# A two-layer diffusion block on one core: the last feed-forward's way down with tokens as weights in four banks, modulation products in runs of four, and a longer matmul in the plan

## The chip, the cores and the metric

The kernel runs on one core of one Trainium2 chip. The metric is the device time in microseconds (us) of one execution; less is better. The profile follows one execution on that core, and its times count from the first instruction.

## The reference, cut to what matters

Two streams of 256 tokens by 1024 features, an image `x` and a context `ctx`, go through two layers. Layer 0 mixes with an mLSTM, layer 1 with neighbourhood attention; each layer then has a gated feed-forward with a short convolution. Shift, scale and gate of each sublayer come from a small product with `ada_w`, the modulation. Only `x` goes through layer 1's feed-forward.

```python
def conv_ffn(h, w_up, b_up, conv_w, conv_b, w_down, b_down):
    u = dwconv(h @ w_up + b_up, conv_w, conv_b)          # 1024 -> 2 x 2816
    a, g = jnp.split(u, 2, axis=-1)
    return (a * jax.nn.silu(g)) @ w_down + b_down          # 2816 -> 1024
...
mod_x = jnp.split((silu_c @ ada_w[i] + ada_b[i])[:, None, :], 6, axis=-1)
hx = modulate(rmsnorm(xx, norm2_g[i]), mod_x[3], mod_x[4])
xx = xx + mod_x[5] * conv_ffn(hx, ...)
...
return rmsnorm(xx, final_g)
```

## The kernel before, in words

**Layout.** Activations lie with features on the partitions and tokens along the free axis: `X[k]` is 128 features by 512 tokens, 256 of `ctx` and 256 of `x`. Float32 accuracy is had from TensorE's one-pass format (fp32r) by splitting each operand into a high and a low part: a cast on ACT writes the high part, a subtraction on DVE the low one (`split`, `split_w`), and `mm3` (line 473) issues three matmuls, high by high, high by low, low by high. A weight tile of 128 by 1024 is loaded to a raw buffer (three of them), cast and subtracted into one of five pairs of buffers. Small products, the modulation among them, are plain float32 matmuls with 32 columns of weights, four side by side on the array (a quad).

**Stages.** First the modulation for norm 1 (`first_scale`, line 505, with rows named `adc`, and `first_shift`, line 526, with rows named `adh`), while the first weights land. Then the mLSTM's projections `u`, its gates, and for each of four heads a front part, the decay matrices, the product `h`, the transposes `ht` (`heads_out`, line 1069) and the way out `wo`; tiles of the projection `z` are put between as filler. Then layer 0's feed-forward on 512 tokens, the attention of layer 1, and layer 1's feed-forward on 256 tokens.

**The modulation.** `ada_steps` (line 545) is a generator: each call of `trickle` does one slice of 128 features. Three of the units go through TensorE (rows `ada<-ra,sc_c`), a quad for each slice, when it has landed; the others are summed on DVE (`aa`) and end in a quad (rows `ada<-aa,esel`).

**The last feed-forward.** `feed_forward` (line 1136) takes the 22 tiles of hidden features in three blocks of 8, 8 and 6. A block is first made (`up` twice for each tile, then convolution taps, a product with silu and a split) and then taken down: for each of 8 output tiles, rows `dn`, weights are the 128 by 128 pieces of `ff_down`, and the hidden tile of 256 tokens moves. The result goes to `X[m]` with bias and gate (`residual`, line 1085). After the last block `finish` (line 1360) scales each output tile, squares it, and turns it with two transposes (`yt`) to tokens on partitions; sums of squares (`pmfin`) give the last norm, and four transfers write the output.

**Who sets the order.** Nothing is issued as written. `Plan.record` keeps each operation with a price (`cost`, line 145) and what it depends on; `group` makes several one. `run` then walks through a planned time with one queue for each engine, picks what is ready and due first, and writes the order down. The prices are fixed numbers, among them:

```python
            if ins[0].dtype == F32R:
                return max(n, 64) / 2.4 + 3, None
            ...
            return 0.833 * n + (52 if psum else 94) + extra, table      # ACT
        return 70 + scalars + (0.52 if fast else 1.04) * n, None        # DVE
```

At run time each engine works through its list in this order and waits where something is missing.

Of the kernel before, what the change touches and what calls it, by code (L numbers as in the profile page):

```python
# [9 lines left out]
F32 = mybir.dt.float32  # L10
F32R = mybir.dt.float32r
AF = mybir.ActivationFunctionType
ALU = mybir.AluOpType
# [44 lines left out]
Z_TILES = (((), (0, 1, 2, 3), (4,)), ((), (5, 6, 7), (8,)), ((), (9, 10, 11), (12,)), ((), (13, 14, 15), ()))  # L58
ADA_VECTOR = {(1, u) for u in range(6)} | {(0, 4)}


class Plan:
# [6 lines left out]
    DMA_RATE = 360.0  # L69
    AHEAD = 100000  # L70
# [14 lines left out]
    def __init__(self, nc, tc):  # L85
# [5 lines left out]
        self.seen = set()  # L91
        self.ops_engine = []
# [56 lines left out]
    def cost(engine, method, outs, ins, kw):  # L149
        n = max([x.free_size() for x in outs[:1] + ins[:1]])  # L150
        psum = any(x.space == bass.MemoryType.PSUM for x in ins)
        if engine == "tensor":
# [3 lines left out]
            if ins[0].dtype == F32R:  # L156
                return max(n, 64) / 2.4 + 3, None
# [22 lines left out]
    def add(self, engine, cost, ins, outs, fns, table, dma=False):  # L180
# [23 lines left out]
        for name, r, _, is_w in acc:  # L204
# [7 lines left out]
                             outs=outs, dma=dma, load=dma and outs[0].space != bass.MemoryType.DRAM))  # L212


    def run(self):
# [83 lines left out]
        while started < n:  # L299
            progress = True  # L300
            while progress:
                progress = False
                for e in avail:
# [32 lines left out]
                    if o["dma"]:  # L336
# [3 lines left out]
                        end = s + c  # L340
# [57 lines left out]
def diffusion_block(ctx: ExitStack, tc: tile.TileContext, I: dict, out: bass.AP):  # L398
# [80 lines left out]

    def split(src, name, n=T):  # L480

        hi = page("h" + name, F32R)
        lo = page("l" + name, F32R)
        nc.scalar.copy(out=hi[:, :n], in_=src)
        nc.vector.tensor_tensor(out=lo[:, :n], in0=src, in1=hi.bitcast(F32)[:, :n], op=ALU.subtract)
        return hi, lo
# [18 lines left out]
    def first_scale(q):  # L505

        ps = bank(f"adc{q}")
        for i in range(4):
            w = page(f"aq{q}{i}")
            load(w, I["ada0c"][q, i])  # L510
            with nc.group():
                for j in range(4):
                    k = i + 4 * (j // 2)
                    nc.tensor.matmul(ps[32 * j:32 * j + 32, :P], sc_c[:, 32 * k:32 * k + 32], w[:, P * j:P * j + P],
                                     start=i == 0, stop=i == 3)
# [10 lines left out]
    def first_shift(half):  # L526

        ps = bank(f"adh{half}")
        for k in range(KD):
            w = page(f"ah{half}{k}")  # L530
            load(w, I["ada0h"][half, k])
            with nc.group():
                for j in range(4):
                    nc.tensor.matmul(ps[32 * j:32 * j + 32, :P], sc_c[:, 32 * k:32 * k + 32],
                                     w[:, P * j:P * j + P], start=k == 0, stop=k == KD - 1)
# [9 lines left out]
    def ada_steps(l, u):  # L545
        ps = bank(f"ada{l}{u}") if (l, u) not in ADA_VECTOR else None
        only = [1] if l == 1 and u > 1 else [0, 1]
        acc = {}
        for k in range(KD):
            if ps is not None:  # L550
                w = raw_w(I["ada"][6 * l + u - 2, k], f"a{l}{u}{k}")
                with nc.group():
                    for j in range(4):
# [806 lines left out]
    def finish(k):  # L1360
# [16 lines left out]
        if k < KD - 1:  # L1377
            turn()
# [153 lines left out]
```

## Time and profile before

| | us |
|---|---|
| three runs | 1193.1, 1193.97, 1194.65 (median 1193.97) |
| the profiled execution's own time | 1195.27 |
| its span, first to last instruction | 1193.1 |
| TensorE (PE) busy | 1173.0 |
| VectorE (DVE) busy | 938.4 |
| ScalarE (ACT) busy | 679.9 |

A matmul's shown time is from its issue to its modelled end, so neighbours overlap; the distance between two starts is what one costs in a row of many. PEld is TensorE's weight load, which runs beside the matmuls. Nearly every instruction has line 137, since the plan issues it there; the names of tiles tell what it is. `sc_c`, `hdn`, `lup` are names of tiles: an `h` or `l` ahead is a high or low part, an `r` a raw load.

### The profile page before, as it was taken

What the parts mean: (1) busy time and instruction counts of PE and PEld (TensorE: products, weight loads), DVE (VectorE), ACT (ScalarE), POOL (GpSimd) and SP (SyncE); (2) the same over time, 40 slices, a digit from 0 to 9 for tenths busy, and PEclk for the clock granted to TensorE, in tenths of its full rate; (3) what the DMA queues carried; (4) which work ended last, traced back from release to release, by engine and by line L of the source; (5) the groups of instructions that cost most, each with busy time, mean ns of one, the idle gap of its engine ahead of it and who ended that gap; (6) DMA issues with size and microseconds to landing.
All of it is one profiled execution on the core that took longest, in us unless ns stands there. A gap on an engine that the chain in (4) does not pass through costs nothing.

```text
span 1193.1 us, 19033 instructions
## 1 busy us (share of the span) xinstructions
PE 1173.0 (98%) x7122; PEld 980.5 (82%) x7122; DVE 938.4 (79%) x1871; ACT 679.9 (57%) x1212; POOL 26.4 (2%) x59
## 2 busy tenths in 40 slices
PE   7999999999999999999999999999999999999997
PEld 4677777888878788878888888888788899999997
DVE  6898678867875699997897667687966879978675
ACT  4465675562735447553455325454857876867473
POOL 0000000000000000000000000000000000000000
PEclk9999999999999999999999999999999999999999
DMA  9647625413344406318457456422432432576552
GB/s 354 248 159 238 185 63 176 141 54 120 119 141 124 151 17 221 107 53 282 132 186 247 135 199 222 145 72 71 116 120 82 161 104 87 173 228 185 182 160 76
DMA packets 68636, 180.05 MB, mean 151 GB/s; under 512 B 8128, under 2 KB 10688, under 8 KB 68544
## 3 DMA queue, kind: packets, MB, share of 16 engines
q1 hardware_dynamic: 68544, 178.84, 46.2%
q8 instruction: 56, 0.92, 0.3%
q14 instruction: 36, 0.29, 0.1%
HBM read 174.61 MB, written 4.19 MB: 150 GB/s over the span
## 4 chain that ended last, share of the span: by engine, by line
PE 78%; issue 16%; DVE 3%; DMA 2%; ACT 1%; SPq 0%; POOL 0%; POOLq 0%; DVEq 0%; ACTq 0%
PE up L137 21%; PE dn L137 10%; PE u L137 8%; PE wo L137 7%; PE z L137 6%; PE k L137 4%; PE va L137 4%; PE h L137 3%; PE q L137 3%; PE sc L137 2%; PE no L137 2%; PE ada L137 2%; PE o L137 1%; PE pt L137 1%; PE s L137 1%
## 5 line engine op out<-in xcount | busy, mean ns | idle before, releaser
L137 PE MATMUL up<-hhn,hup 128*128 128x512 f32 (+1 forms) x640 | 215.9, 337 | 0.0
L137 PE MATMUL up<-hln,hup 128*128 128x512 f32 (+1 forms) x640 | 215.3, 336 | 0.3 <-DVE hln L137 0.3
L137 PE MATMUL up<-hhn,lup 128*128 128x512 f32 (+1 forms) x640 | 215.1, 336 | 0.0
L137 ACT CAST hup<-rup 128x1024 fp32r<-128x1024 f32 x80 | 83.7, 1050 | 128.6 <-PE up L137 64.7
L137 PEld LDWEIGHTS up<-hhn,hup 128*128 128x128 f32 x640 | 121.5, 190 | 14.0 <-issue 0.8
L137 PEld LDWEIGHTS up<-hln,hup 128*128 128x128 f32 x640 | 121.5, 190 | 12.8 <-DVE hln L137 0.5
L137 PEld LDWEIGHTS up<-hhn,lup 128*128 128x128 f32 x640 | 121.5, 190 | 12.5
L137 DVE TENSOR_TENSOR lup<-rup,hup 128x1024 fp32r<-128x1024 f32 x80 | 97.4, 1223 | 39.6 <-ACT hup L137 39.1
L137 PE MATMUL dn<-hhid,hdn 128*128 128x512 f32 (+1 forms) x352 | 119.3, 339 | 0.0
L137 PE MATMUL dn<-hhid,ldn 128*128 128x512 f32 (+1 forms) x352 | 118.4, 336 | 0.0
L137 PE MATMUL dn<-lhid,hdn 128*128 128x512 f32 (+1 forms) x352 | 118.4, 336 | 0.0
L137 DVE SCALAR_TENSOR_TENSOR fc<-fu,vec,fc 128x510 f32<-128x510 f32 (+1 forms) x176 | 104.6, 612 | 4.8 <-ACT fc L137 4.0
L137 DVE SCALAR_TENSOR_TENSOR aa<-ra,sc_c,aa 128x512 f32<-128x512 f32 x140 | 97.5, 745 | 4.5 <-DMA ra<-in_ada 4.3
L137 ACT CAST hdn<-rdn 128x1024 fp32r<-128x1024 f32 (+1 forms) x48 | 46.6, 979 | 46.5 <-PE up L137 27.1
L137 PEld LDWEIGHTS dn<-hhid,hdn 128*128 128x128 f32 x352 | 66.8, 190 | 7.6 <-issue 0.8
L137 PEld LDWEIGHTS dn<-hhid,ldn 128*128 128x128 f32 x352 | 66.8, 190 | 7.3 <-DVE ldn L137 0.4
L137 PEld LDWEIGHTS dn<-lhid,hdn 128*128 128x128 f32 x352 | 66.8, 190 | 6.9 <-DVE lhid L137 0.2
L137 DVE TENSOR_TENSOR ldn<-rdn,hdn 128x1024 fp32r<-128x1024 f32 (+1 forms) x48 | 54.2, 1133 | 18.5 <-ACT hdn L137 18.3
L137 ACT CAST hw<-rw 128x1024 fp32r<-128x1024 f32 (+1 forms) x36 | 34.0, 952 | 54.1 <-DMA rw<-in_w_in 45.4
L137 PE MATMUL wo<-ly,hwo 128*128 128x512 f32 x128 | 50.8, 397 | 3.5 <-DVE ly L137 3.5
L137 ACT ACTIVATE fc<-up,cb,vec 128x512 f32<-128x512 f32 (+1 forms) x80 | 53.1, 664 | 0.0
L137 PE MATMUL z<-hhn,hw 128*128 128x512 f32 x128 | 51.4, 402 | 0.0
(349 smaller groups left out, 2777.0 us busy)
## 6 DMA issues: line engine op xcount, KB each, us to landing
rup<-in_ff_up SPq DMA_DIRECT2D x80, 512.0 KB, 4.1
ra<-in_ada SPq DMA_DIRECT2D x112, 256.0 KB, 5.6
rdn<-in_ff_down SPq DMA_DIRECT2D x32, 512.0 KB, 3.6
rw<-in_w_in SPq DMA_DIRECT2D x28, 512.0 KB, 4.0
ra<-in_ada SPq DMA_DIRECT2D x24, 512.0 KB, 4.4
rwo<-in_w_out SPq DMA_DIRECT2D x16, 512.0 KB, 3.7
rdn<-in_ff_down SPq DMA_DIRECT2D x16, 384.0 KB, 3.2
aq<-in_ada0c SPq DMA_DIRECT2D x16, 256.0 KB, 5.2
```

Of the source, the lines that this page charges most:

```text
L137: fn = lambda: getattr(getattr(self.nc, engine), method)(*args, **kw)
```

## The change

Six edits go together.

1. `last_feed_forward` takes the place of `feed_forward(1, ...)` and of `finish`. The hidden tile's 128 tokens become the weights and 512 columns of `ff_down` (now laid out as 22 tiles of 128 by 1024, `ff_last`) move. Two halves of the tokens by two halves of the features make four banks that stay open through all 22 tiles; tile `j - 4` goes down after tile `j` is made, and the last three tiles bank by bank. `X` is turned once at the start (`xt`), gate, bias and the last norm's weights are laid out as rows, and the end needs no transposes. The gate's row is made by writing 128 by 8 numbers to DRAM (`gd`) and reading them back to all partitions (`grow`).
2. `two_parts`: where a pair has 256 columns, both halves share a page (names `bhid`, `bhn`, `ben`).
3. Modulation quads are made into groups of four slices (`ADA_GROUP`): `adh`, `ada` and, but for the first, `adc`. The weights come as pages of 256 KB, no longer as raw buffers.
4. The quads of `gates`, `wsn` and `o` become one group each.
5. In `Early` the scaled input `etn` is made on ACT, no longer on DVE.
6. The plan's price of an fp32r matmul goes from 3 to 13.3 ns over the columns' time, and a DMA to or from `gd` is planned 6 us longer.

```diff
@@ Plan.cost @@
             if ins[0].dtype == F32R:
-                return max(n, 64) / 2.4 + 3, None
+                return max(n, 64) / 2.4 + 13.3, None
@@ first_shift @@
-        for k in range(KD):
-            w = page(f"ah{half}{k}")
-            load(w, I["ada0h"][half, k])
+        for k0 in range(0, KD, ADA_GROUP):
+            ws = []
+            for k in range(k0, k0 + ADA_GROUP):
+                ws.append(page(f"ah{half}{k}"))
+                load(ws[-1], I["ada0h"][half, k])
             with nc.group():
-                for j in range(4):
-                    nc.tensor.matmul(ps[32 * j:32 * j + 32, :P], sc_c[:, 32 * k:32 * k + 32],
-                                     w[:, P * j:P * j + P], start=k == 0, stop=k == KD - 1)
+                for k, w in enumerate(ws, k0):
+                    for j in range(4):
+                        nc.tensor.matmul(ps[32 * j:32 * j + 32, :P], sc_c[:, 32 * k:32 * k + 32],
+                                         w[:, P * j:P * j + P], start=k == 0, stop=k == KD - 1)
@@ ada_steps @@
-                w = raw_w(I["ada"][6 * l + u - 2, k], f"a{l}{u}{k}")
-                with nc.group():
...
+                w = [page(f"ra{l}{u}{k}{i}") for i in range(2)]
+                for i in range(2):
+                    load(w[i], I["ada"][6 * l + u - 2, k][:, 512 * i:512 * i + 512])
+                held.append((k, w))
+                if len(held) == ADA_GROUP:
+                    with nc.group():
...
@@ Early @@
-                    nc.vector.tensor_scalar(out=t[:, S * i:S * i + S], in0=X[k][:, S * s:S * s + S], scalar1=A[i][:, k:k + 1],
-                                            scalar2=None, op0=ALU.mult)
+                    nc.scalar.activation(out=t[:, S * i:S * i + S], in_=X[k][:, S * s:S * s + S], func=AF.Copy,
+                                         scale=A[i][:, k:k + 1])
@@ in place of feed_forward(1, ...) and finish @@
+        def down(j, i, hf):
+            if j not in W:
+                W[j] = split_w(I["ff_last"][j], f"dn{l}{j}")
...
+            mm3(acc[i][hf], cut(hid[j], P * i, P * i + P), cut(W[j], 512 * hf, 512 * hf + 512), j == 0, j == KF - 1)
...
+        LAG = 4
+        TAIL = 3
+        for j in range(KF):
+            hid.append(ffn_hidden(l, S, j, up(j, 0), up(j, 1)))
+            if LAG <= j < KF - TAIL - 2 + LAG:
+                for x in BANKS:
+                    down(j - LAG, *x)
+            if j == 5:
...
+                nc.sync.dma_start(out=gd.rearrange("k p -> p k"), in_=gs)
...
+                    load(g, gd[4 * hf:4 * hf + 4, :].rearrange("k p -> (k p)")[None, :].broadcast_to([P, 512]))
+                    nc.vector.tensor_tensor(out=bd, in0=bd, in1=g, op=ALU.mult)
...
+        def ends(i, hf):
+            y[i, hf] = t, sq, _ = page(f"yf{i}{hf}"), page(f"sqf{i}{hf}"), page(f"yg{i}{hf}")
+            nc.vector.tensor_tensor(out=t, in0=acc[i][hf], in1=rows[hf][0], op=ALU.mult)
+            nc.vector.tensor_tensor(out=t, in0=t, in1=rows[i, hf], op=ALU.add)
+            nc.scalar.activation(out=sq, in_=t, func=AF.Square, scale=1.0 / 32, accum_out=ss[:, i, hf:hf + 1])
...
```

The plan writes a new order for every engine. Three places of it follow.

On PE, in the projection `u` at the start, before: quads of `first_shift` (`adh`; x4 is one quad) stand one or two at a time between three matmuls of `u`.

```order
L137 MATMUL adh_193<-ah_199,sc_c 32x128 x4
L137 MATMUL u_169<-hn_113,hw_172 128x512
L137 MATMUL u_169<-ln_114,hw_172 128x512
L137 MATMUL u_169<-hn_113,lw_173 128x512
L137 MATMUL adh_193<-ah_200,sc_c 32x128 x4
L137 MATMUL u_169<-hn_116,hw_172 128x512
L137 MATMUL u_169<-ln_117,hw_172 128x512
L137 MATMUL u_169<-hn_116,lw_173 128x512
L137 MATMUL adh_193<-ah_201,sc_c 32x128 x4
L137 MATMUL adh_204<-ah_205,sc_c 32x128 x4
```

The same place with the change (`rbn` is the norm's broadcast):

```order
L140 MATMUL u_148<-hn_176,hw_151 128x512
L140 MATMUL u_148<-ln_177,hw_151 128x512
L140 MATMUL u_148<-hn_176,lw_152 128x512
L140 MATMUL rbn_183<-dln_187,onesr 128x256
L140 MATMUL rbn_188<-dhn_191,onesr 128x256
L140 MATMUL adh_193<-ah_198,sc_c 32x128 x4
L140 MATMUL adh_193<-ah_199,sc_c 32x128 x4
L140 MATMUL adh_193<-ah_200,sc_c 32x128 x4
L140 MATMUL adh_193<-ah_201,sc_c 32x128 x4
```

Four quads stand in a row. Counted over the whole list, stretches between fp32r matmuls that hold quads of `adh` go from 11 to 4, those with `ada` from 28 to 12, those with `adc` from 5 to 3; the number of quads is the same.

On PE, at the end of the mLSTM's first head, before: 21 matmuls of `z`, the last four transposes `ht`, two small transposes, nine matmuls of the next head's `q` (left out here) and two of `gb`, and then the way out `wo`, whose second matmul reads the low part `ly`.

```order
L137 MATMUL z_521<-hhn_229,lw_524 128x512
L137 MATMUL ht_509<-con,hn_483 128x128
L137 MATMUL ht_512<-con,hn_483 128x128
L137 MATMUL ht_515<-con,hn_483 128x128
L137 MATMUL ht_518<-con,hn_483 128x128
L137 MATMUL adat_527<-con,adas_526 128x128 x2
...
L137 MATMUL gb_624<-ghl,pairr 128x512
L137 MATMUL wo_542<-hy_510,hwo_540 128x512
L137 MATMUL wo_542<-ly_511,hwo_540 128x512
```

With the change all 16 transposes stand ahead of 24 matmuls of `z` (all but the first two and the last left out):

```order
L140 MATMUL ht_534<-con,hn_488 128x128
L140 MATMUL ht_534<-con,hn_495 128x128
L140 MATMUL z_537<-hhn_215,hw_539 128x512
L140 MATMUL z_537<-lhn_216,hw_539 128x512
...
L140 MATMUL z_537<-hhn_229,lw_540 128x512
L140 MATMUL adat_543<-con,adas_542 128x128 x2
L140 MATMUL wo_558<-hy_526,hwo_556 128x512
L140 MATMUL wo_558<-ly_527,hwo_556 128x512
```

On SP, whose list holds every transfer, in the last feed-forward with the change: the write of `gd`, and six transfers later the first read of it (`grow`), which waits for the write to land, with weight tiles (`rup`, `rdn`) between and behind.

```order
L140 DMA gd<-gs 128x8x1
L140 DMA brow_2545<-in_rows 128x512
L140 DMA frow_2546<-in_rows 128x512
L140 DMA rdn_2603<-in_ff_last 128x1024
L140 DMA rup_2611<-in_ff_up 128x1024
L140 DMA rup_2617<-in_ff_up 128x1024
L140 DMA grow_2544<-gd 128x512
L140 DMA rdn_2623<-in_ff_last 128x1024
```

Before, only weight tiles stand there, `rup` ahead of a block and `rdn` behind it:

```order
L137 DMA rup_2725<-in_ff_up 128x1024
L137 DMA rup_2731<-in_ff_up 128x1024
L137 DMA rdn_2738<-in_ff_down 128x1024
L137 DMA rdn_2742<-in_ff_down 128x1024
L137 DMA rdn_2746<-in_ff_down 128x1024
```

## Rows read from the trace of the kernel before

**Rows 1.** The page's head and its first part: busy time, share of the span and number of instructions of each engine.

```profile
span 1193.1 us, 19033 instructions
PE 1173.0 (98%) x7122; PEld 980.5 (82%) x7122; DVE 938.4 (79%) x1871; ACT 679.9 (57%) x1212; POOL 26.4 (2%) x59
```

**Rows 2.** Busy time by stretch: the stretch, its length, then us and number of instructions for each engine, PE's granted clock, the share of the DMA engines, GB/s.

```profile
0.00:60.00 60.00, 52.25 (x472) 34.07 (x473) 47.22 (x119) 28.02 (x52) 4.22 (x16) 1.00 0.81 299
60.00:1184.40 1124.40, 1119.57 (x6644) 945.55 (x6642) 888.76 (x1748) 650.16 (x1158) 21.50 (x42) 1.00 0.45 143
412.00:437.00 25.00, 23.71 (x99) 19.35 (x100) 22.35 (x53) 12.85 (x24) 0.00 (x0) 0.93 0.00 1
988.00:1042.00 54.00, 53.60 (x492) 52.85 (x491) 51.54 (x114) 42.08 (x81) 1.87 (x1) 1.00 0.42 129
1042.00:1172.00 130.00, 130.00 (x1086) 130.00 (x1085) 96.17 (x151) 82.69 (x140) 0.00 (x0) 1.00 0.62 186
```

**Rows 3.** The chain of work that ended last, one piece in layer 0's feed-forward: start, us, what, number of matmuls (512 columns each).

```profile
571.13 27.20 PE up L137 x120
```

**Rows 4.** Groups by form: the last way down's first product, number, busy us, mean ns, idle before.

```profile
L137 PE MATMUL dn<-hhid,hdn 128*128 128x256 f32 x176 | 50.3, 286 | 0.0
```

**Rows 5.** Timeline of PE in the last way down, where a pair of `yt` transposes stands between: start, us, what.

```profile
1180.82 0.28 PE L137 MATMUL dn<-hhid,ldn 128*128 128x256 f32 x1
1180.94 0.38 PE L137 MATMUL yt<-con,xf 128*128 128x128 f32 x2
1181.08 0.36 PE L137 MATMUL dn<-hhid,hdn 128*128 128x256 f32 x1
1181.28 0.28 PE L137 MATMUL dn<-lhid,hdn 128*128 128x256 f32 x1
```

**Rows 6.** Timeline of PE around one quad of the modulation (a float32 matmul is two instructions, so x8).

```profile
57.97 0.39 PE L137 MATMUL u<-hhn,lw 128*128 128x512 f32 x1
58.29 0.64 PE L137 MATMUL ada<-ra,sc_c 128*32 128x256 f32 x8
58.86 0.50 PE L137 MATMUL u<-hhn,hw 128*128 128x512 f32 x1
59.20 0.39 PE L137 MATMUL u<-hln,hw 128*128 128x512 f32 x1
```

**Rows 7.** The same around two quads in a row.

```profile
509.03 0.39 PE L137 MATMUL up<-hhn,lup 128*128 128x512 f32 x1
509.35 1.07 PE L137 MATMUL ada<-aa,esel 128*32 128x256 f32 x16
...
510.69 0.40 PE L137 MATMUL up<-hln,hup 128*128 128x512 f32 x1
```

**Rows 8.** The same around one quad of `first_shift`, whose columns are 128.

```profile
40.70 0.40 PE L137 MATMUL u<-hn,lw 128*128 128x512 f32 x1
41.02 0.42 PE L137 MATMUL adh<-ah,sc_c 128*32 128x128 f32 x8
...
41.71 0.39 PE L137 MATMUL u<-ln,hw 128*128 128x512 f32 x1
```

**Rows 9.** Timeline of PE where the first head's way out begins; in brackets the idle time and who ended it.

```profile
196.96 0.39 PE L137 MATMUL wo<-hy,hwo 128*128 128x512 f32 x1
199.25 0.50 PE L137 MATMUL wo<-ly,hwo 128*128 128x512 f32 x1 [1.90 <-DVE ly L137]
```

**Rows 10.** The same where the last head's way out begins.

```profile
411.19 0.49 PE L137 MATMUL wo<-hy,hwo 128*128 128x512 f32 x1
413.29 0.50 PE L137 MATMUL wo<-ly,hwo 128*128 128x512 f32 x1 [1.60 <-DVE ly L137]
...
414.13 0.63 PE L137 MATMUL wo<-ly,hwo 128*128 128x512 f32 x1
```

**Rows 11.** Groups by form on DVE and ACT: number, busy us, mean ns, idle before and who ended it.

```profile
L137 DVE TENSOR_TENSOR lup<-rup,hup 128x1024 fp32r<-128x1024 f32 x80 | 97.4, 1223 | 39.6 <-ACT hup L137 39.1
L137 ACT CAST hup<-rup 128x1024 fp32r<-128x1024 f32 x80 | 83.7, 1050 | 128.6 <-PE up L137 64.7 <-PE dn L137 37.6 <-issue 10.5
L137 ACT ACTIVATE hhn<-etn,mp 128x256 fp32r<-128x256 f32 x40 | 17.2, 499 | 2.7 <-DVE etn L137 2.6
L137 DVE TENSOR_SCALAR etn<-xr,An 128x256 f32<-128x256 f32 x40 | 12.5, 346 | 0.0
```

**Rows 12.** Timeline of the end, from the last matmul of the way down to the transfers of the output.

```profile
1184.12 0.28 PE L137 MATMUL dn<-hhid,ldn 128*128 128x256 f32 x1
...
1186.60 0.69 POOL L137 TENSOR_TENSOR rsfin<-msfin,mhalf 128x2 f32<-128x2 f32 x1 [186.82 <-DVE msfin L137]
1187.33 1.27 ACT L137 ACTIVATE r<-yt,rsfin 128x512 f32<-128x512 f32 x2 [1.88 <-POOL rsfin L137]
1187.33 1.41 DVE L137 TENSOR_SCALAR r<-yt,rsfin 128x512 f32<-128x512 f32 x2 [0.81 <-POOL rsfin L137]
1188.04 1.81 SPq L137 DMA_DIRECT2D out_y<-r  x4
```

**Rows 13.** DMA issues: number, KB each, us from issue to landing (median). `gb` is 128 pieces of 4 bytes.

```profile
ra<-in_ada SPq DMA_DIRECT2D x112, 256.0 KB, 5.6
gb<-in_gb SPq DMA_DIRECT2D x1, 0.5 KB, 6.2
```

More of the change, by code (lines that the diff above doesn't have):

```diff
@@ L69 @@
     DMA_RATE = 360.0
+    DMA_ROWS = 6000
     AHEAD = 100000
@@ L507, in first_scale @@
         ps = bank(f"adc{q}")
+        ws = []
         for i in range(4):
[L509 to L510 removed]
+            ws.append(page(f"aq{q}{i}"))
+            load(ws[i], I["ada0c"][q, i])
+        runs = [range(4)] if q else [(i,) for i in range(4)]
+        for run in runs:
             with nc.group():
[L512 to L515 removed]
+                for i in run:
+                    for j in range(4):
+                        k = i + 4 * (j // 2)
+                        nc.tensor.matmul(ps[32 * j:32 * j + 32, :P], sc_c[:, 32 * k:32 * k + 32],
+                                         ws[i][:, P * j:P * j + P], start=i == 0, stop=i == 3)
         sb = half_page(f"adcs{q}")
@@ L674, in shift_terms @@
         pc = bank(f"ws{name}")
-        for k in range(KD):
-            with nc.group():
+        with nc.group():
+            for k in range(KD):
                 for j in range(4):
@@ L876, in diffusion_block @@
                 continue
-            for src, gwt in ((UC, guc), (U, gu)):
-                with nc.group():
+            with nc.group():
+                for src, gwt in ((UC, guc), (U, gu)):
                     for j in range(4):
@@ L1175, in up, with ffn_hidden, feed_forward @@
             return acc
+        return up
+    def ffn_hidden(l, n, j, a, g):
+        sg = page(f"sg{l}{j}")
+        nc.scalar.activation(out=sg[:, :n], in_=g[:, :n], func=AF.Silu)
+        pr = page(f"pr{l}{j}")
+        nc.vector.tensor_tensor(out=pr[:, :n], in0=a[:, :n], in1=sg[:, :n], op=ALU.mult)
+        return split(pr[:, :n], f"hid{l}{j}", n)
+    def feed_forward(l, streams, after):
+        ns = len(streams)
+        n = S * ns
+        name = f"n2{l}"
+        ms = [0, KF, 1, KF + 1]
+        early = Early(l, 1, streams, name, [I["ff_up"][l, m] for m in ms], [(0, n)] * 4, [f"up{l}{m}" for m in ms])
+        h = norm_pages(name, n)
+        norm_rest(l, 1, early, h)
+        up = ffn_up(l, streams, early, ms, h)
         for q in range(3):
@@ L1323, in attend @@
         po = bank(f"o{m}")
-        for s in range(4):
-            with nc.group():
+        with nc.group():
+            for s in range(4):
                 for e in range(2):
@@ L1381, in diffusion_block @@
-    feed_forward(1, [1], lambda m: last.append(finish(m)))
-    pm = bank("pmfin")
-    for i in range(2):
-        for x in range(2):
-            nc.tensor.matmul(pm[:, i:i + 1], sums["fin", x][:, P * i:P * i + P], ones[:, 0:1], start=x == 0, stop=x == 1)
-    last[-1]()
-    ms = nc.tile(sm, [P, 2], F32, "msfin", "ms", 4)
-    nc.vector.tensor_scalar(out=ms, in0=pm[:, 0:2], scalar1=1.0 / 1024, scalar2=EPS, op0=ALU.mult, op1=ALU.add)
-    rs = nc.tile(sm, [P, 2], F32, "rsfin", "rs", 4)
-    nc.gpsimd.tensor_tensor(out=rs, in0=ms, in1=mhalf[:, :2], op=ALU.pow)
@@ L1401, in diffusion_block @@
+    last_feed_forward()
     nc.run()
```

148 lines of the change are left out of this document (96 added, 52 removed).

## The prediction

> **What bounds the kernel now.** I read the page's head first: PE is busy for 98% of the span, no other engine for more than 79% [rows 1]. Then the busy time by stretch: from 60 to 1184.4 us PE is idle for 1124.40 - 1119.57 = 4.8 us in all, at full clock as a mean; only before 60 us, where the DMA engines are 81% busy, and after the last matmul is there more [rows 2]. So a gain must take time out of PE's own list, fill one of its few waits, or shorten the ends, and whatever DVE, ACT or the queue do comes free until PE waits for it. The chain of waits gives the price of PE's common instruction: 120 matmuls of 512 columns in 27.20 us, 0.2267 each [rows 3]. The stretch of the last feed-forward gives the other: 1086 of 256 columns in 130.00 us, 0.1197 each [rows 2]. Both are about 13 ns over the columns at the 2.4 GHz that a clock row of 1.00 stands for.
>
> The sum below is made against the profiled execution's own time, 1195.27, which is 1.30 above the median of the runs.
>
> **Longer matmuls in the last way down: -3.4.** Before it is three products of 176 matmuls each [rows 4], 528 x 0.1197 = 63.2 us. The same work with 512 columns moving is 264 x 0.2267 = 59.8.
> A rule of the Trainium skill speaks against this term. Its page "TensorE: Matmul & The Clock Gate", section "Back-to-back issue gap", puts a matmul at its columns over 2.4 and about 2.5 ns. By that the term would be an estimate of 264 x 2.5 ns = 0.7 instead of 3.4; the rows on this kernel's format show 13 ns, and I go by them.
>
> **Fewer changes between quads and fp32r: -7.9.** A quad between two matmuls of `u` makes their distance 59.20 - 57.97 = 1.23 us; less two pitches it costs 0.78 [rows 6]. Two quads in a row cost 510.69 - 509.03 - 0.453 = 1.21 [rows 7]. The second thus costs 0.43, and 0.35 is paid once for each stretch of quads. A quad of `adh` with half the columns costs 41.71 - 40.70 - 0.453 = 0.56 [rows 8]; less half of 0.43 that leaves 0.34, the same fixed price. The order has 16 stretches fewer with `ada` (16 x 0.345 = 5.5) and 7 fewer with `adh` (2.4). The two fewer of `adc` lie in the start, which the transfers bound, and count nothing (at most 0.7). The groups of `gates`, `wsn` and `o` count nothing: the order before already has these quads together.
>
> **The stall at the first head's way out: -2.1.** The second matmul of `wo` waits for `ly`: 199.25 - 196.96 - 0.227 = 2.06 us [rows 9]. In the new order 24 matmuls of `z` stand between the last `ht` and `wo`, 24 x 0.2267 = 5.4 us of work, where nine of `q` and two of `gb` stood, 2.5 us. 2.9 more cover the 2.06. Next late could be only `hwo`, a weight with a long lead. The last head's stall, 413.29 - 411.19 - 0.227 = 1.87 [rows 10], has no such filler and stays, with the lower clock behind it (0.93 over 25 us [rows 2], single matmuls of 0.63 [rows 10]).
>
> **The scaled inputs move from DVE to ACT: 0.** 40 instructions of 0.346 leave DVE (13.8 us), and on ACT, by the nearest row, they are 0.499 each, 20 us [rows 11]. Before the last feed-forward ACT has 42.08 busy of 54; eight more make 46.1 [rows 2]. There PE has 53.60 of 54, so nothing is to be had. At 412 to 437 us DVE is the fuller engine, 22.35 of 25 [rows 2]: that is a rival's case.
>
> **The shared pages and the last feed-forward's balance: 0.** The weights' casts and subtractions have the same columns as before, 22 x 1024 on either engine. In 1042 to 1172 us DVE is busy for 96.17 of 130 and ACT for 82.69 [rows 2]. A hidden tile now takes 48 x 0.1197 + 12 x 0.2267 = 8.5 us of PE; DVE spends about 6.3 in that time at the old rate. The six new products and sums of rows with 512 columns are at most 6 x 1.22 = 7.3 us by the row of the subtraction [rows 11], against 33.8 idle. The 16 new transposes `xt` take the place of 16 `yt`, a pair of which costs 1181.28 - 1180.82 - 0.24 = 0.22 [rows 5]: 0, within 0.5. Their four copies go to ACT and nobody waits for them before the end.
>
> **The end: -0.4.** From the last `dn` at 1184.12 to the last `r` at 1188.74 it takes 4.6 us, then four issues of 0.45, the last done 1.1 after that `r` [rows 12]. Now the last bank needs two DVE passes (0.70 each, as `r`), a square (0.63), a small sum, the power (0.69), and `r` (0.70) [rows 12], about 3.9 with the matmul's own 0.28 and some 0.5 for hand-overs; only two transfers are then left to issue. I take -0.4, between -1 and +1.
>
> **The start: +0.7.** The new list of transfers has three pages of 256 KB ahead of the first tile of the projection's weights, since the first product waits for a whole run. At 299 GB/s [rows 2] that is 0 to 2.6 us of delay; the last tiles of the stretch keep their places, so I take a quarter.
>
> **A new plan with other prices: +1.5.** The plan now takes a 512-column matmul for 226.6 ns, which is what it is [rows 3], where 216.3 stood. But it still takes a cast for 947 where the row says 1050, and a subtraction for 1135 where it is 1223 [rows 11]. Before, all three were too cheap by 5 to 10%, and kept their proportion; now it sees ACT and DVE earlier, against PE, than they will be. So it puts less filler in: in one place of the attention's front 13.4 us of PE work stand where 15.1 stood. Such thinning costs between 0 (the cover was ample) and about 6, if each of some four heads and two fronts loses as much as one of today's stalls, below 2.06 and 1.87. Less than nothing is possible too where the truer price orders better. I take 1.5, a third of today's 4.8 idle.
>
> **Sum.** -3.4 - 7.9 - 2.1 - 0.4 + 0.7 + 1.5 = -11.6: 1195.27 becomes 1183.7, and against the median 1193.97 becomes **1182.4**.
>
> **The rivals.**
> A, the forecast, with sizes off by some us: 0.66, 1179 to 1186.
> B, the relieved DVE brings `ly` earlier also in the last head. For it: DVE was 22.35 of 25 there. Against it: the order still has `wo` right behind `ht`. It gives the 1.87 and the low clock's price, (1 - 0.93) x 25 = 1.75 us: 1178.8. Chance 0.07.
> C, the thinner filler lets PE wait for casts and subtractions in the fronts, in the way of the stalls of rows 9 and 10 and with the lower clock behind each, 3.6 apiece; two or three of them, 6 to 11 over the sum: 1188 to 1193. For it: the planned prices; against it: only two stalls of that size in the whole trace before. 0.13, of which 0.06 stays faster and 0.07 comes within the bound below.
> D, the 13 ns go with the columns rather than with the instruction, or the longer matmul meets something else, so that two pitches of 0.1197 make one of the new: the first term is 0, 1185.8. Against it: 0.2267 in the chain for 512 columns. The page's rule named above lies close to this case, with 0.7 in place of 0. 0.03.
> E, the fixed 0.35 of a stretch isn't spared, since PE would wait for a landing or a bank in most of those places anyway (a group of four waits for all eight pages): 1182.4 + 7.9 = 1190.3. Against it: hardly any idle stands in those places before. 0.05.
> F, slower. The write of `gd` is 1024 pieces of 4 bytes, and only when it has landed can `grow` be read; SP, which issues in order, waits there with the next weight tiles behind it. The nearest row of tiny pieces is `gb`, 128 of them, 6.2 us; a page of 256 KB takes 5.6 [rows 13]. So the write takes from 5.6 (pieces cost nothing) to 8 x 6.2 = 49.6 (eight times the pieces, eight times the time). I take 6.2: the page with 512 times the bytes is no slower than `gb`, so most of that is common to any transfer. DVE needs the product of `brow` and `grow` two hidden tiles, 17 us, after it has written `gs`; if `grow`, 5.6 more, is late, the subtractions queued behind stop. Five pairs of split tiles, three to a hidden tile, then carry PE for 5/3 x 8.5 = 14 us. So PE starves from a landing of 17 + 14 - 5.6 = 25 us on; at 49.6 it loses 24: 1206. It is slower than before by more than can be told from a landing of about 39 us. 0.06.
>
> **The numbers.** A measurement of this kernel can tell about 0.2%, 2.4 us. Faster by more than that: A, B, D, E and the better part of C, 0.66 + 0.07 + 0.03 + 0.05 + 0.06 = 0.87. Within it: the rest of C, 0.07. Slower: F, 0.06. The range leaves out most of C's far half, part of E, F and a little on the low side. Its low end is the sum without the +2.2 of start and plan and with B's 3.6: 1182.4 - 5.8 = 1176.6, say 1176. Its high end takes the plan's upper bound, the start's and the end's: 4.5 + 1.9 + 1.4 = 7.8, 1190.2, say 1190.
>
> **What will show it.** Right steps: 264 matmuls `dn` of 512 columns at 0.227; between fp32r matmuls, `ada` rows of x32 (four quads) that cost 0.35 + 4 x 0.43 = 2.07 in a row instead of 3.1; no idle ahead of the first `wo<-ly`; idle of PE from 60 us to the last matmul about 4 us; clock rows of 1.00 but behind the last head. After the last `dn`, 8.6 us or so. Wrong steps: a release by ACT or DVE ahead of `u`, `qk` or `up` of 1 us and more (C); the pitch of `dn` at 0.24 (D); idle of the DMA kind ahead of `ada` or `adh` (E); the landing of `gd` above 20 us, with SP waiting on it and idle of PE ahead of `up` and `dn` (F). A slower start shows as PE busy below 52.25 in the first 60 us.

## The result and the profile after

The changed kernel takes 1184.73 us (median of four runs, 1183.17 to 1185.46) where the kernel before took 1193.66 beside it: a ratio of 0.9921, with a 95% interval from 0.9907 to 0.9935, some 9 us. The prediction was 1182.4, between 1176 and 1190. The profiled execution took 1184.44 with a span of 1182.7. Against the profiled one of before, which lay above its median, that is 10.8 less, and the span is 10.4 shorter; the account below is of these 10.4.

The head of the page after, as [rows 1]:

```profile
span 1182.7 us, 18560 instructions
PE 1160.3 (98%) x6850; PEld 967.6 (82%) x6850; DVE 926.8 (78%) x1810; ACT 689.9 (58%) x1245; POOL 29.4 (2%) x60
```

Busy time by stretch, columns as in [rows 2], the stretches moved by the time gained up to them:

```profile
0.00:60.00 60.00, 51.56 (x475) 36.43 (x476) 45.96 (x118) 30.63 (x55) 4.36 (x16) 1.00 0.97 345
60.00:1174.40 1114.40, 1108.18 (x6375) 931.12 (x6375) 877.42 (x1687) 656.47 (x1185) 24.19 (x43) 1.00 0.45 143
403.00:428.00 25.00, 24.23 (x107) 20.00 (x108) 22.76 (x48) 19.79 (x40) 0.00 (x0) 1.00 0.00 0
1032.00:1162.00 130.00, 129.55 (x914) 121.79 (x913) 96.35 (x144) 83.13 (x138) 0.00 (x0) 1.00 0.67 193
```

PE's idle time between 60 us and its last matmul is 1114.40 - 1108.18 = 6.2 us, more than the 4.8 of before, although a stall of 2 us went away. So something else was lost. The clock row behind the last head is 1.00, where it was 0.93. To see where time was won and lost, read off when the same work begins in each trace (start in us; the third and fourth columns belong to two experiments below):

| event on PE | before | after | after, old price | before, new price |
|---|---|---|---|---|
| first `u` | 11.29 | 13.46 | 13.21 | 10.96 |
| first `q` | 132.91 | 128.38 | 127.87 | 132.21 |
| second head's `sc` | 220.95 | 213.50 | 213.15 | 221.47 |
| last head's `wo` | 411.19 | 401.89 | 400.66 | 410.65 |
| layer 0's first `dn` | 527.09 | 515.65 | 514.44 | 524.36 |
| attention's first `k` | 807.25 | 795.30 | 794.10 | 804.25 |
| last feed-forward's first `up` | 990.80 | 982.48 | 978.57 | 993.04 |
| last `dn` | 1184.12 | 1174.52 | 1168.05 | 1188.13 |
| end of the span | 1193.1 | 1182.7 | 1176.2 | 1197.1 |

Up to the attention the change is 12.0 us ahead. By the last feed-forward it has only 8.3 left, so 3.6 were given back in the attention alone, where the change rewrites little but the order. Then the new way down and the end bring 2.1 more.

What the main steps look like now. Runs of four quads on PE; the first three rows answer to [rows 8], the last to [rows 6, 7]:

```profile
40.85 0.40 PE L140 MATMUL u<-hn,lw 128*128 128x512 f32 x1
41.18 1.08 PE L140 MATMUL adh<-ah,sc_c 128*32 128x128 f32 x32
42.52 0.39 PE L140 MATMUL u<-ln,hw 128*128 128x512 f32 x1
...
330.81 1.91 PE L140 MATMUL ada<-ra,sc_c 128*32 128x256 f32 x32
```

Four quads of `adh` cost 42.52 - 40.85 - 0.453 = 1.22 us where one costs 0.56 [rows 8]: 0.22 for each further one, so that 0.34 is paid once here too. The way out of the first head, answering to [rows 9]:

```profile
188.54 0.39 PE L140 MATMUL z<-hhn,lw 128*128 128x512 f32 x1
...
188.90 0.48 PE L140 MATMUL wo<-hy,hwo 128*128 128x512 f32 x1
189.22 0.39 PE L140 MATMUL wo<-ly,hwo 128*128 128x512 f32 x1
```

The second `wo` follows the first in 0.32: no wait, and `z` stands ahead, as the order had it. The last head still waits for `ly`, as in [rows 10], but at full clock behind it:

```profile
401.89 0.49 PE L140 MATMUL wo<-hy,hwo 128*128 128x512 f32 x1
403.77 0.50 PE L140 MATMUL wo<-ly,hwo 128*128 128x512 f32 x1 [1.38 <-DVE ly L140]
404.11 0.40 PE L140 MATMUL wo<-hy,lwo 128*128 128x512 f32 x1
```

The last way down by form, answering to [rows 4], 176 + 88 = 264 matmuls of 512 columns:

```profile
L140 PE MATMUL dn<-hdn,bhid 128*128 128x512 f32 x176 | 57.4, 390 | 0.0
L140 PE MATMUL dn<-ldn,bhid 128*128 128x512 f32 x88 | 34.5, 392 | 0.0
```

Their mean of 390 ns is issue to end; the starts lie 0.227 apart. The end, answering to [rows 12]:

```profile
1174.52 0.39 PE L140 MATMUL dn<-hdn,bhid 128*128 128x512 f32 x1
...
1177.69 0.55 POOL L140 TENSOR_TENSOR rsfin<-msfin,mhalf 128x1 f32<-128x1 f32 x1 [2.93 <-DVE msfin L140]
...
1178.28 0.75 DVE L140 SCALAR_TENSOR_TENSOR r<-yf,rsfin,frow 128x512 f32<-128x512 f32 x1 [0.67 <-POOL rsfin L140]
```

From the last `dn` to the last `r` it is 4.5 us (before 4.6), and from there to the end 1182.7 - 1179.03 = 3.7 (before 4.4), since two of the four transfers have gone by then: 0.85 in all.

### The profile page after: what moved, and what is told of

It is laid out like the page before. It is cut to its first block, busy times and chain, and to the rows that moved or that the text cites. A ratio compares the mean times of both kernels' runs of the same rounds, so it can differ in the third digit from the quotient of the medians.

```text
span 1182.7 us, 18560 instructions
## 1 busy us (share of the span) xinstructions
PE 1160.3 (98%) x6850; PEld 967.6 (82%) x6850; DVE 926.8 (78%) x1810; ACT 689.9 (58%) x1245; POOL 29.4 (2%) x60
## 4 chain that ended last, share of the span: by engine, by line
PE 82%; DVE 7%; ACT 5%; DMA 4%; issue 2%; SPq 0%; POOL 0%; POOLq 0%; ACTq 0%; DVEq 0%
PE up L140 28%; PE dn L140 14%; PE z L140 7%; PE wo L140 7%; PE u L140 4%; PE va L140 4%; PE sc L140 3%; PE h L140 3%; PE k L140 2%; PE q L140 2%; DMA rup<-in_ff_up 2%; DVE uc L140 1%; PE v L140 1%; PE ada L140 1%; DMA aq<-in_ada0c 1%
## 5 line engine op out<-in xcount | busy, mean ns | idle before, releaser
L140 PE MATMUL up<-hhn,hup 128*128 128x512 f32 x320 | 125.4, 392 | 0.0
L140 PE MATMUL up<-hhn,lup 128*128 128x512 f32 x320 | 124.6, 389 | 0.0
L140 PE MATMUL up<-lhn,hup 128*128 128x512 f32 x320 | 124.6, 389 | 0.0
L140 PE MATMUL up<-bhn,hup 128*128 128x256 f32 x640 | 116.9, 284 | 0.8 <-ACT fc L140 0.5
L140 PEld LDWEIGHTS up<-bhn,hup 128*128 128x128 f32 x640 | 100.9, 192 | 2.8 <-ACT fc L140 0.7
L140 PE MATMUL up<-bhn,lup 128*128 128x256 f32 x320 | 90.5, 283 | 0.0
L140 DVE TENSOR_TENSOR ldn<-rdn,hdn 128x1024 fp32r<-128x1024 f32 (+1 forms) x46 | 54.0, 1176 | 25.7 <-ACT hdn L140 25.6
L140 PEld LDWEIGHTS up<-hhn,hup 128*128 128x128 f32 x320 | 60.1, 188 | 13.9 <-issue 0.8
L140 PE MATMUL dn<-hhid,hdn 128*128 128x512 f32 x176 | 68.9, 391 | 0.0
L140 PE MATMUL dn<-hhid,ldn 128*128 128x512 f32 x176 | 68.5, 389 | 0.0
L140 PE MATMUL dn<-lhid,hdn 128*128 128x512 f32 x176 | 68.5, 389 | 0.0
```

The costliest lines, as they stand in the source:

```text
L140: fn = lambda: getattr(getattr(self.nc, engine), method)(*args, **kw)
```

## The experiments

Ratios and medians are against the kernel before, run beside each; differences in the traces are against the trace of the kernel that was edited. The runs of the kernel before had medians from 1193.7 to 1194.9 beside the different experiments, so medians of two experiments compare to about 1 us.

**The plan's price, taken back.** The place of the loss points at the order, and the attention's order differs through the price, the groups of `o` and, in its front, the scaled input. Taking the edits back one at a time tells them apart. First the price:

```diff
-                return max(n, 64) / 2.4 + 13.3, None
+                return max(n, 64) / 2.4 + 3, None
```

> The changed kernel with the plan's old price of an fp32r matmul (3 ns over its columns in place of 13.3), all else as changed. From the start of layer 1's attention to the first up of the last feed-forward the change lost 5.3 us against before, 12.0 gained up to there becoming 6.7. Theory one (the new price thins the filler): most of it comes back, 3 to 5 us, among it the wait of PE for the exponentials at 841 us (2.05 us, before 0.69); the heads stay as they are: 1180 to 1182. Theory two (the loss comes from quads of o being one group of sixteen): at most 1 us comes back there, 1184 to 1186, and where the old price lets PE run ahead of ACT and DVE in the heads a stall of 1 to 2 us may return. Theory three (the scaled input on ACT makes ACT late): nothing comes back, 1184.7.

Measured: 1177.93, ratio 0.9862 (0.9849 to 0.9876), 6.8 us less than the changed kernel and the fastest of all that ran. The wait for the exponentials is as before: 0.69 from start to start less a pitch, where the changed kernel has 2.05. In the traces the difference is 6.5. The new order costs more than the whole first term of the prediction. What the price moved can be seen at the wait of PE in the attention. PE after, and with the old price (one fence for each):

```profile
839.38 0.39 PE L140 MATMUL s<-kl,qq 128*128 128x512 f32 x1
841.66 0.50 PE L140 MATMUL k<-hhn,hk 128*128 128x512 f32 x1 [1.89 <-ACT pe L140]
```

```profile
838.15 0.39 PE L140 MATMUL s<-kl,qq 128*128 128x512 f32 x1
839.07 0.50 PE L140 MATMUL k<-hhn,hk 128*128 128x512 f32 x1 [0.53 <-ACT pe L140]
```

`k` needs the bank that `s` occupies until ACT has read it (`pe`), ACT needs the row maximum `nmx`, and DVE makes it. DVE after:

```profile
836.63 0.42 DVE L140 TENSOR_REDUCE mx<-s 128x1 f32<-128x256 f32 x1 [1.41 <-PE s L140]
837.31 1.23 DVE L140 TENSOR_TENSOR lwv<-rwv,hwv 128x1024 fp32r<-128x1024 f32 x1 [0.25 <-ACT hwv L140]
838.45 0.42 DVE L140 TENSOR_REDUCE mx<-s 128x1 f32<-128x256 f32 x1
...
839.52 0.15 DVE L140 TENSOR_SCALAR nmx<-mx 128x1 f32<-128x1 f32 x1
```

The same with the old price:

```profile
835.41 0.88 DVE L140 TENSOR_REDUCE mx<-s 128x1 f32<-128x256 f32 x2 [0.71 <-PE s L140]
...
836.94 0.14 DVE L140 TENSOR_SCALAR nmx<-mx 128x1 f32<-128x1 f32 x1
```

With the new price one subtraction of a weight, `lwv`, stands between the first two maxima. It takes 1.23 us, after 0.25 of waiting for its own cast, and PE's wait is 1.36 longer. No filler became thinner here: an instruction that nobody needed yet was put into the chain that PE waits for.

The front of the last feed-forward, 1.8 of the loss, is the same. PE's `up<-bhn` needs `bhn`, made from `etn`. DVE after has two subtractions of weights, `lup`, ahead of it, with the old price one (one fence for each):

```profile
992.60 2.58 DVE L140 TENSOR_TENSOR lup<-rup,hup 128x1024 fp32r<-128x1024 f32 x2
995.10 1.42 DVE L140 TENSOR_TENSOR etn<-etn,rsn 128x256 f32<-128x256 f32 x4
```

```profile
987.90 1.22 DVE L140 TENSOR_TENSOR lup<-rup,hup 128x1024 fp32r<-128x1024 f32 x1
989.03 1.42 DVE L140 TENSOR_TENSOR etn<-etn,rsn 128x256 f32<-128x256 f32 x4
```

The other part of the 1.8 is 0.6 around a wait for `wssn`: on DVE a subtraction `len21up` of 0.68 stands ahead of it, with the old price behind it, and there PE doesn't wait. One place is the other way round, and there the filler is thinner: behind the last `s` of the attention, 33 matmuls `no` stand ahead of the transposes `pt`, with the old price 42. The first `pn` is then ready 6.52 us after those `s` began, with the old price only after 7.02, and yet PE waits in the changed kernel alone (after, then with the old price):

```profile
958.58 1.32 PE L140 MATMUL pt<-con,pn 128*128 128x128 f32 x8 [0.60 <-DVE pn L140]
```

```profile
956.10 1.33 PE L140 MATMUL pt<-con,pn 128*128 128x128 f32 x8
```

So of the 6.5 some 3.2 are instructions put ahead of one that PE waits for (1.36, 0.6 and about 1.2), and 0.6 is thinner filler. The rest, 1.2 up to layer 0's feed-forward, 0.7 behind the last front and small pieces, I didn't follow to a cause.

**The groups of `gates`, `wsn` and `o`, taken back.**

```diff
-        with nc.group():
-            for s in range(4):
+        for s in range(4):
+            with nc.group():
```

> The changed kernel with the quads of gates, wsn and o in groups as before, all else as changed. Theory one (price): nothing comes back, 1184.7, within 1. Theory two (one group of o): its order in the attention then differs from before only by the price, and 2 to 3 of the 5.3 us lost between the attention's start and the last feed-forward come back, above all the 1.19 us in the stretch of the output projection with its wait of 0.76 for pn: 1182 to 1183. For the heads both say the same as in the changed kernel, within 0.3.

Measured: 1184.09, ratio 0.9919 (0.9905 to 0.9933): no difference from the changed kernel that can be told. The attention's order then differs from that of before through the price and the scaled input alone, and the wait of 2.05 is still there. Theory two falls.

**The scaled input back on DVE.**

```diff
-                    nc.scalar.activation(out=t[...], in_=X[k][...], func=AF.Copy, scale=A[i][:, k:k + 1])
+                    nc.vector.tensor_scalar(out=t[...], in0=X[k][...], scalar1=A[i][:, k:k + 1], scalar2=None, op0=ALU.mult)
```

> The changed kernel with the scaled input made on DVE again. The order on PE is the same but for one broadcast. Theory A (the stall at the last head's way out and the low clock behind it depend on DVE's load there): the stall goes from 1.65 back to about 1.87 and the granted clock of the 25 us behind it back from 1.00 to 0.93, 1.8 us in all: 1186.5. Theory B (they depend on the order alone): both stay, 1184.7. Theory three (ACT late in layer 1's fronts): the 0.55 us of the attention's front and the wait for wssn ahead of the last feed-forward go, 1 to 2 us less: 1183 to 1183.7 if B holds too.

Measured: 1185.48, ratio 0.9925 (0.9912 to 0.9937), 0.75 more than the changed kernel and less than can be told from nothing. The stall at the last head's way out stays 1.65 and the clock behind it full, so theory A falls. In the trace 0.34 of the attention's front come back, less than theory three had. The wait of `k` for the exponentials is the same, 1.89 in brackets, but half clock follows it here: the twelve `k` behind it take 1.2 us more. Without that this trace would be 0.25 shorter than the changed kernel's.

**The last feed-forward as before.** `feed_forward(1, ...)` and `finish` in place of `last_feed_forward`, with `ff_down` for both layers.

> The changed kernel with the last feed-forward and the end as before (528 matmuls of 256 columns in its way down, transposes of the result), edits 2 to 6 kept. By the stage account the new way down gave 3.51 in the matmuls' pitch, gave back 1.1 net in the transposes at its start and 0.8 in new short waits, and the end gave 0.85. So without it 2.5 to 3.5 us slower than the changed kernel: 1187 to 1188. If the pitch of 512 columns with tokens as weights brought nothing (rival D): within 1 of 1184.7. If the new last feed-forward is what makes the front before it slow (1.66 us lost there): 1186.

Measured: 1189.21, ratio 0.9958 (0.9945 to 0.9970), 4.5 us more than the changed kernel. In the trace 4.4: the matmuls' pitch 3.5, the end 0.86, and the rest cancels. I had expected less, since I put the 1.1 us of transposes at the start of the new one against it; the old one has as much in its own transposes and in short waits.

**The price alone, in the kernel before.** The first diff above, the other way round, in the old kernel.

> The kernel before with one edit, the price of an fp32r matmul 13.3 in place of 3 ns over its columns. In the changed kernel taking this edit back gave 6.5 us: 0.5 at the start, 0.9 in the heads, 3.2 in layer 1's attention up to the last feed-forward's front with 1.8 there, the rest behind it. Theory one (the price alone thins the filler, whatever else is changed): the attention and the front lose 3 to 5 here as well, and the wait for the exponentials becomes 2.05 in place of 0.69; the first head's way out gets 24 matmuls of z ahead of it, which takes its stall of 2.06 away: in sum 1195 to 1197. Theory two (the loss needs the grouped quads or ACT's scaled input): the attention stays, and with the stall gone 1191 to 1192.

Measured: 1199.14, ratio 1.0032 (1.0020 to 1.0044): slower, by 4.5 us. So the price does it whatever else is changed, and by more than I gave it. Its column in the table shows where: ahead up to the attention by 3.0, since the first head's stall and the low clock go, and then 7 us are lost, 5.2 of them in the attention. The wait for the exponentials on PE is about that of the changed kernel, with the same `lwv` between the maxima on DVE, and half clock behind it adds 1.6 here:

```profile
846.09 1.23 DVE L137 TENSOR_TENSOR lwv<-rwv,hwv 128x1024 fp32r<-128x1024 f32 x1 [0.41 <-ACT hwv L137]
...
848.00 0.39 PE L137 MATMUL s<-kl,qq 128*128 128x512 f32 x1
850.43 0.50 PE L137 MATMUL k<-hhn,hk 128*128 128x512 f32 x1 [2.05 <-ACT pe L137]
```

**All prices as measured.** If what matters is how the engines' prices stand to each other, raising those of ACT and DVE to the rows should mend it.

```diff
-            return 0.833 * n + (52 if psum else 94) + extra, table
+            return 0.833 * n + (152 if psum else 194) + extra, table
...
-        return 70 + scalars + (0.52 if fast else 1.04) * n, None
+        return 155 + scalars + (0.52 if fast else 1.04) * n, None
```

> The changed kernel with the plan's prices of ACT and DVE raised as well: 100 ns on each ACT instruction and 85 on each of DVE, so that a cast of 1024 columns costs 1047 (measured 1050) and a subtraction 1220 (measured 1219), beside the matmul's 13.3. Theory one in the form of the prediction (what matters is the proportion of the engines' prices): the 6.5 us of the old price come back for the most part, 1178 to 1180, the wait for the exponentials below 1 us. Rival (each new set of prices gives another order, good or bad, and the old price was lucky): no better than 1183, with new waits elsewhere.

Measured: 1205.43, ratio 1.0089 (1.0075 to 1.0103), some 20 us more than the changed kernel. This speaks clearly against theory one in the form of the prediction. PE's waits in all (us, times, longest) have other and larger ones ahead:

```profile
PE dn L140 <- DVE lhid L140: 4.3, 3, 2.2
PE wo L140 <- DVE ly L140: 4.2, 3, 2.0
PE sc L140 <- DVE lq L140: 3.5, 1, 3.5
```

The constants were fitted to instructions of 1024 columns and put on all. They fit others too: the scaled input of 256 columns on DVE is then planned at 348 ns and measured 346 [rows 11]. Whether another fit would do better wasn't tried.

**Two more prices**, 8 in place of 13.3, and 7 below the columns.

> The changed kernel with the price at 8 ns over the columns, midway between the old 3 (1177.9) and the new 13.3 (1184.7). Theory one (the higher PE is priced, the less filler stands ahead of its waits, gradually): about midway, 1180 to 1183. Rival (each price gives one order, good or bad, with no trend): anything from 1178 to 1190.

Measured: 1183.53, ratio 0.9905 (0.9892 to 0.9919).

> The changed kernel with the price at 7 ns under the columns, so that PE is as much underpriced against the measured rows (9% at 512 columns) as the casts are. Theory one with a trend: 1174 to 1178, waits for ACT and DVE at most as in the kernel with the old price. The rival (no trend, the old price's order was a good one): 1179 or more, with waits in the heads or the attention.

Measured: 1190.33, ratio 0.9964 (0.9952 to 0.9977). Over the price, -7, 3, 8, 13.3, the times are 1190.3, 1177.9, 1183.5, 1184.7: from 3 up it gets slower, as theory one has it, but at -7 too, by 12 us, where theory one with a trend forecast 1174 to 1178. The old value is the best of the four. At 8 the wait for the exponentials is short (0.69), but the first head's `wo` waits again for 1.4 and the last front loses 2.7 against the old price; at -7 the first head waits twice and layer 0's `dn` for `lhid`. The rival fits these four better: a price gives an order, and orders are good or bad.

**One slice to a group of the modulation.**

```diff
-ADA_GROUP = 4
+ADA_GROUP = 1
```

> The changed kernel with one slice to a group in the modulation (ADA_GROUP = 1 in place of 4), pages and all else as changed. Some 23 stretches of quads more between fp32r matmuls. If each stretch has the fixed price of 0.345: 7.6 us slower in the start and the heads, 1192. If PE waits for landings anyway and the price isn't spared (rival E): 1185 to 1187. If pages instead of raw buffers made part of the gain, less than 7.6 by that part.

Measured: 1193.57, ratio 0.9991 (0.9981 to 1.0002), 8.8 more than the changed kernel. In the trace 19 more stretches of other work up to layer 0's feed-forward cost 6.3 us together with the late matmul behind each, 0.33 a stretch. The rest is a new wait of 1.7 for `lq` in the second head, and 1.6 behind the wait for the exponentials: the wait is that of the changed kernel, but half clock follows it. PE, the stretch, and the same stretch in the changed kernel:

```profile
850.08 0.50 PE L140 MATMUL k<-hhn,hk 128*128 128x512 f32 x1 [1.89 <-ACT pe L140]
...
852.39 0.63 PE L140 MATMUL k<-lhn,hk 128*128 128x512 f32 x1
```

```profile
848.50:873.50 25.00, 23.42 (x169) 18.37 (x170) 18.70 (x70) 20.64 (x58) 2.08 (x7) 0.93 0.33 96
```

```profile
840.00:865.00 25.00, 23.34 (x176) 18.53 (x177) 19.94 (x80) 22.26 (x64) 2.09 (x7) 1.00 0.35 105
```

So the fixed price is real, rival E falls, and nothing shows that the pages in place of raw buffers gave anything of their own. This run also shows the stall at the last head's way out without the low clock, PE and then the stretch behind:

```profile
409.58 0.49 PE L140 MATMUL wo<-hy,hwo 128*128 128x512 f32 x1
411.68 0.50 PE L140 MATMUL wo<-ly,hwo 128*128 128x512 f32 x1 [1.61 <-DVE ly L140]
412.02 0.40 PE L140 MATMUL wo<-hy,lwo 128*128 128x512 f32 x1
```

```profile
410.00:435.00 25.00, 23.39 (x105) 19.23 (x105) 23.41 (x48) 19.21 (x39) 0.00 (x0) 1.00 0.02 8
```

**Groups of eight, with the old price.**

```diff
-ADA_GROUP = 4
+ADA_GROUP = 8
...
-                return max(n, 64) / 2.4 + 13.3, None
+                return max(n, 64) / 2.4 + 3, None
```

> The kernel with the old price (1177.9) and groups of eight slices in the modulation in place of four. Some five stretches of quads fewer at 0.345 each: 1.7 us faster, 1176.2, if a stretch's price is fixed and nothing waits. Rival: a group of eight waits for 16 pages, and PE idles for a landing ahead of adh or ada, or pages run short for others: 1178 to 1181. The attention's order is the same, so it should take the same time within 0.2.

Measured: 1196.53, ratio 1.0016 (1.0008 to 1.0025), 18.6 more than with groups of four. Neither theory: no landing and no page is waited for. The attention is the same within 0.2, the start is 1.2 faster between `u` and `q`, and then one place of the first head loses 18, since the order has `mt` right behind `gf`, with nothing to cover the gates' scans between. The wait is 11.7, and from 147.5 to 156 us the granted clock is 0.53:

```profile
134.77 1.12 PE L140 MATMUL gf<-gsb,con 128*128 128x512 f32 x2 [0.73 <-ACT gsb L140]
...
147.62 0.44 PE L140 MATMUL mt<-con,gM 64*128 64x64 f32 x2 [11.73 <-DVE gM L140]
```

**More pieces in the write of `gd`.** In the changed kernel it landed after 11.0 us and `grow` after 8.1. The queue waited 2.3 us for the write, PE for neither:

```profile
grow<-gd SPq DMA_DIRECT2D x2, 256.0 KB, 8.1
gd<-gs SPq DMA_DIRECT2D x1, 4.0 KB, 11.0
```

```diff
-                gd = dr.tile([KD, P], F32, name="gd")
-                gs = nc.tile(sm, [P, KD], F32, "gs", "A", 4)
-                nc.vector.tensor_copy(out=gs, in_=mgate[l][1][:, :, 1])
+                gd = dr.tile([8 * KD, P], F32, name="gd")
+                gs = nc.tile(sm, [P, 8 * KD], F32, "gs", "gs", 1)
+                for r8 in range(8):
+                    nc.vector.tensor_copy(out=gs[:, KD * r8:KD * r8 + KD], in_=mgate[l][1][:, :, 1])
```

> The changed kernel with gd written eight times over, 8192 pieces of 4 bytes in the one transfer in place of 1024; grow reads the same bytes as before. The order on PE is the same. In the changed kernel the write landed after 11.0 us, where 128 pieces took 6.2: 5.4 ns a piece more. Rival F's mechanism: landing 50 us, grow 8 us later, DVE stops at the first product with grow and PE starves from a landing of 25 us on: 25 us lost, 1210. If a piece costs nothing and the 11 is a fixed price of the form: 1184.7. If landing is 50 but the split tiles and banks cover more than I counted: 1185 to 1200, with PE idle ahead of up.

Measured: 1199.56, ratio 1.0037 (1.0027 to 1.0048). It landed after 24.8 us, about 2 ns a piece more and not 5.4, and the span is 13.2 longer. The queue's timeline shows another mechanism than the one I wrote down:

```profile
1031.17 0.38 SPq L140 DMA_DIRECT2D gd<-gs  x1
1031.60 15.97 SPq L140 DMA_DIRECT2D brow<-in_rows  x1
...
1049.95 0.38 SPq L140 DMA_DIRECT2D rdn<-in_ff_last  x1
...
1055.95 0.33 SPq L140 DMA_DIRECT2D grow<-gd  x1
```

The issue of the transfer behind `gd` takes 16 us; in the changed kernel it took 0.57, and `rdn` was issued at 1033.07. The weight tiles come that much later, and `dn` waits 11.2 us for the cast of one, with half clock behind the wait. `grow` isn't what is waited for. I repeated it with four times the pieces:

> The changed kernel with gd written four times over, 4096 pieces of 4 bytes. Written eight times over it landed after 24.8 us, but what cost 13 us was another thing: SP's next transfer took 16 us to issue right behind it, and the weight tiles came late. If that queue takes a certain number of pieces and the rest wait: about 7 us of issue, landing about 17, and up to 3 us lost, 1184.7 to 1188. If the issue is held for as long as the pieces last: 8 us and 4 to 5 lost. If up to 4096 go in at once: nothing, 1184.7.

Measured: 1191.63, ratio 0.9974 (0.9965 to 0.9983). The issue behind takes 6.17 us and the landing 15.0, nearest to the first of the three forecasts, though with more than its 3 us lost: the trace's span is 3.6 longer, and the median is 6.9 above the changed kernel's, so this profiled execution was one of the shortest.

## Why the prediction was right

The total lies in the range and near the forecast, but partly because two errors went against each other.

- **Longer matmuls, -3.4:** 3.5 in the account of the pitches, and 4.5 as an experiment with the end. Right. By the rule of the Trainium skill that was set against it ("TensorE: Matmul & The Clock Gate", section "Back-to-back issue gap"), which the page gives for an isolated matmul, an estimate would have been 0.7. The pitch of 0.227 on this format decides, and rival D falls.
- **Fewer changes, -7.9:** summed over the stretches of other work between fp32r matmuls up to layer 0's feed-forward, waits left out, the time beyond the neighbouring pitches fell by 6.8 us, and that of the late matmuls behind by 1.8: 8.6. That is as much as 0.345 for each of 16 + 7 + 2 stretches, with the two of `adc` that the prediction counted as nothing. Right, and borne out by groups of one.
- **The first head's stall, -2.1:** gone, with 24 matmuls of `z` ahead. Right in size. But the new price alone took it away in the old kernel, and the other edits do with the old price, so it can't be credited to one of them.
- **The last head's stall and the low clock, 0:** wrong. The wait went from 1.87 to 1.65 and the low clock vanished, 1.8 together. That was half of rival B, but not by its mechanism: with the scaled input back on DVE both are the same. Most of it may be luck of the execution: with one slice to a group a wait of 1.87 had full clock behind it, and the runs of the kernel before that stood beside the later experiments have mean granted clocks from 0.995 to 0.999.
- **Scaled inputs, shared pages:** 0 forecast; a median of 0.75 for the first, of which the trace shows half clock behind one wait and no gain, and nothing seen of the second.
- **The end, -0.4:** -0.85, inside its bounds. From the last `dn` to the last `r` it was 4.5 and not 3.9; the pieces that the prediction lists add up to 4.2.
- **The start, +0.7:** the first `u` came 2.2 later, yet the first `q` 4.5 earlier, in a start whose DMA engines are now 97% busy. The delay was caught up. I can't separate the two further.
- **The new price, +1.5:** the step that failed. It costs 6.8 us as measured by taking it back, so even its upper bound of 6 was low; in the kernel before it costs 4.5 by the medians, and in the trace 3.0 are won and 7 lost. The reason given, thinner filler from prices out of proportion, explains 0.6 of it, at `pt`; and prices in proportion were some 20 us worse. In its place the traces show subtractions of weights on DVE put ahead of what PE waits for, in three places that make 3.2 of the 6.5; some 2.7 stay open.
- **The write of `gd`:** landing 11.0 against the 6.2 I took, without harm. The rival's mechanism was wrong: at 24.8 us, where I said that PE starves from 25 on, 13 us were already lost, by the held-up queue.

Summed: -3.5 - 8.6 - 2.1 - 1.8 - 0.85 = -16.9, of which the new order gave back the 6.5 of its trace, which gives the span's -10.4. So close a sum is partly chance, since each piece is good to a few tenths and the start isn't in it. Without the price edit the same kernel reaches 1177.93.

## What to carry to other kernels

In a kernel whose order a planner writes, an edit of a price is an edit of every place: cost it by the new order, engine by engine, at the places where the bounding engine waits, and look there for an instruction that was moved ahead of the one waited for, and then for filler that went. Truer prices need not give a better order, so measure such an edit by itself, never in one bundle with edits that remove work. Costs that are paid on each change of the kind of work can be read from two neighbouring rows (one in a row, two in a row), and hold.

## What the runs showed of the hardware

- One change from fp32r matmuls to quads with 32 columns of weights and back costs 0.34 to 0.35 us, whatever the number of quads between: one and two quads of 256 columns cost 0.77 and 1.21 in all, three (with one slice to a group) 1.63; one, four and eight quads of 128 columns (eight with groups of eight) 0.56, 1.22 and 2.08.
- A write of 1024 pieces of 4 bytes lands in 11.0 us, and the next transfer on the queue takes 0.57 us to issue; with 4096 pieces it lands in 15.0 and the next takes 6.2, with 8192 in 24.8 and 16.
- The same work with the same wait of 1.87 us ahead of `wo` was followed by a granted clock of 1.00 in one kernel and 0.93 in another [rows 2, 10]: half speed, 1.2 GHz, in single rows of 0.63. The wait of 1.89 ahead of `k` was likewise followed by 1.00 in the changed kernel and by 0.93 with one slice to a group. The length of the wait alone doesn't decide it, and what does stays open.
